# Four small PE steps of a planned transformer layer are queued some products later

## The chip, the cores and the metric

The kernel runs on one core of a Trainium2 chip. Its engines work side by side, each through a queue of its own in the order in which the program wrote it: PE (TensorE, matrix products; its weight loads are listed apart as PEld), DVE (VectorE), ACT (ScalarE), POOL (GpSimd), and SP (SyncE), which issues most of the transfers from and to HBM. An engine waits on a semaphore where an instruction needs another engine's result, and everything behind that instruction in its queue waits too. The metric is the device time of one execution in microseconds (us); lower is better.

## The reference, cut to what matters

One layer over 512 tokens of width 2048, all in float32:

```
h    = rms_norm(x, norm1_g) * (1 + sc1) + sh1            # sc1, sh1, ... = silu(c) @ w_ada + b_ada
proj = h @ w_in                                          # q, k, v, iq, ik, iw | r, k, v, w, a, g
att  = dsa_sparse_attention(...)    # 8 heads; a score picks the top 128 keys of each query
rwkv = rwkv7_time_mix(...)          # 16 heads of 64; a recurrent state over the 512 tokens
x    = x + gt1 * (concat(att, rwkv) @ w_out)
h2   = rms_norm(x, norm2_g) * (1 + sc2) + sh2
out  = x + gt2 * ((silu(h2 @ w_ffn_gate) * (h2 @ w_ffn_up)) @ w_ffn_down)
```

The queries and keys of the attention, and the keys of the recurrence, are normalised per head, which needs a sum of squares over a head's 128 or 64 columns.

## The kernel before, in words

**The big products.** Activations lie transposed (features on partitions, 512 tokens along a row). Each weight tile is split into a high part `whi` (cast by ACT) and a low part `wlo` (difference by DVE), each activation likewise, and three products (high by high, low by high, high by low) go into one sum `acc` (or `vacc`). A list of jobs gives these main products: the projections by `w_in`, then `w_out`, then the three FFN matrices. Before each job `run_jobs` (line 266) has SP load a tile three jobs ahead, and ACT and DVE split half tiles four ahead. The program holds 10032 main products; below, "main product 1086" counts them in program order.

**The planner.** All else is written as generators, the *streams*: `prep` (line 650, eight pairs of recurrent heads), `solve` (780, on DVE), `scan` (826), `post` (914), the rest of the `w_ada` product on DVE (967, tile `wad`), the key score and its top-k on DVE (1066, `idx_stream`), `norm_qk` (1138) and the heads (1168). `drive` (line 288) lets the job list write three main products, then gives each stream a turn. A planner with a clock per engine estimates when each tile will be ready; a stream that calls `until(tile)` gets no further until the planner's PE clock has passed that estimate plus `SLACK`, 0.5. So the planner, on estimates, decides behind how many main products a small PE step stands. Where a job may not be written yet, nothing but streams is written.

**The steps of the change.** `colsum` (line 525) sums columns on DVE: a STREAM_TRANSPOSE into `tr`, a TENSOR_REDUCE into `sums`. `spread` (531) brings the sums across partitions by small PE products into `pst`. `prep` does so once for each of 8 pairs, `norm_qk` once for each of 16 q and k heads, with a rope on DVE between the sums and the products. `prep` later builds `work` on DVE and transposes it on PE (`pT`). `scan` goes through 8 chunks of 64 tokens for each of two groups of heads, and each chunk needs the one before: PE makes `p1` from the chunk's tiles `ch` and the state `SSd`; ACT and DVE copy it into `Rs`; PE makes `p2` from `Rs` and `tt`; DVE and ACT copy that into `ch`; PE makes `p3` and the output `po`; DVE adds `p3` to the state `S` and makes the next `SSd`. In the profile p1, p2 and p3 are all called `p`, told apart by what they read: `p<-SSd,arc` and `p<-ch` with it (p1), `p<-R,tt` (p2), `p<-ch x16` right ahead of `po` (p3).

**The gate on the q and k jobs.** Attention heads start only when the scan of both groups has ended and the top-k is done. Until then at most four (later six) q and k tiles may wait:

```
1265    def few():
1266        return len(qk) <= (6 if len(scanned) == 2 else 4)
1269            group_T(win, h * 128, TWO, ALLK, 4, hrhs, evac_qk("q", h), need=few)
```

The tiles q0, q1, k0, k1, q2 and q3 make six, so the job behind main product 2448 is not written until the scan has ended. The `w_out` jobs behind main product 3048 need all heads.

Of the kernel before, what the change touches and what calls it, by code (L numbers as in the profile page):

```python
# [48 lines left out]
def layer_kernel(ctx, tc, x, c, positions, w_ada, b_ada, norm1_g, w_in, q_norm_g, k_norm_g,  # L49
# [8 lines left out]
    ready = {}  # L58
# [4 lines left out]
    def nm(ap):  # L63
        t = getattr(ap, "tensor", None)
        return getattr(t, "name", None)
# [67 lines left out]
    def now():  # L133
        return clk["pe"]

    SLACK = 0.5
    PACE1, PACE, PACE2 = 3.6, 1.9, 3.0

    def until(*aps):

        t = max(ready.get(nm(a), 0.0) for a in aps) + SLACK
        while now() < t:
            yield

    def room(key="dve", lim=3.0):
        while clk[key] - now() > lim:
            yield

    def banks(n):

        while True:
            for k in [k for k, v in psread.items() if v is not None and v <= now()]:
                del psread[k]
            if len(psread) + n <= 4 and side["pe"] <= SIDE:
                return
            yield
# [16 lines left out]
    def G(name="g", dt=F32):  # L173
        return gpool.tile([128, 512], dt, name=name, tag="g")

    def B(name="b", dt=F32):
        return bpool.tile([128, 2048], dt, name=name, tag="b")
# [4 lines left out]
    def SM(name="sm"):  # L182
        return spool.tile([128, 16], F32, name=name, tag="sm")
# [4 lines left out]
    def PS(name="ps"):  # L188
        t = psp.tile([128, 512], F32, name=name, tag="ps")
        psread[nm(t)] = None  # L190
        return t

    def mm(o, l, r, start=True, stop=True):
        PE.matmul(o, l, r, start=start, stop=stop)
# [187 lines left out]
    def ada_take(kind, c0, k):  # L382
        while (kind, c0, k) not in ada_t:
            yield
        t, last = ada_t.pop((kind, c0, k))
        yield from until(t)
        return t, last
# [137 lines left out]
    def colsum(dst, t):  # L525

        u = G("tr")
        V.transpose(u, t)
        V.tensor_reduce(dst, u.rearrange("p (b c) -> p b c", c=32), axis=mybir.AxisListType.X, op=OP.add)

    def spread(ps, parts, col=C_MOD):

        pv = parts.rearrange("p (j a) -> p a j", a=4)
        for a in range(4):
            mm(ps[32 * a:32 * a + 32], cst[:, col:col + 32], pv[:, a, :])
# [114 lines left out]
    def prep(j):  # L650
# [15 lines left out]
        sm = SM("sums")  # L666
# [1 line left out]
        sg, at = G("sg"), G("at")  # L668
        A.activation(sg, pw, AF.Tanh, scale=0.5, bias=der[:, D_HW + j:D_HW + j + 1])
        A.activation(at, pa, AF.Tanh, scale=0.5, bias=der[:, D_HA + j:D_HA + j + 1])  # L670
        yield from until(sm)
        yield from banks(1)
        pst = PS("pst")
        for h in range(2):
# [35 lines left out]
        work = B("work").rearrange("p (u f) -> p u f", f=1024)  # L710
# [11 lines left out]
        V.tensor_tensor(BK[:, :, 1, :], v3(kf), v3(e2), op=OP.mult)  # L722
        SP.dma_start(ars[:, :, j, :].rearrange("c p f -> p c f"), work[:, 0, :].rearrange("p (c f) -> p c f", f=128))
        V.scalar_tensor_tensor(rt, rt, v2[:, R_RK + j:R_RK + j + 1], kf, op0=OP.mult, op1=OP.mult)
        yield from until(work)
        BKf = work[:, 1, :].rearrange("p (c f) -> p c f", f=128)
        ARf = work[:, 0, :].rearrange("p (c f) -> p c f", f=128)
        for half in range(2):
# [97 lines left out]
    def scan(g):  # L826
# [8 lines left out]
        def load(cI):  # L835
            ch = B("ch").rearrange("p (j f) -> p j f", f=512)
            ar = G("arc")
            hs = slice(cI % 2 * 64, cI % 2 * 64 + 64)
            SP.dma_start(ch[:, :, 0:384], pk[cI, :, js, 0:384])
            SP.dma_start(ch[64:128, :, 384:512], pk[cI, 64:128, js, 384:512])  # L840
            P.memset(ch[0:64, :, 384:512], 0.0)
            SP.dma_start(ar.rearrange("p (j f) -> p j f", f=128), ars[cI, :, js, :])
            SP.dma_start(tt[hs].rearrange("s (q t) -> s q t", t=C), xts[g, :, cI * 8:cI * 8 + 8, :])
            loads[cI] = ch, ar.rearrange("p (j f) -> p j f", f=128)
# [3 lines left out]
        SSd, tt, Rs = G("SSd"), G("tt"), G("R")  # L848
# [5 lines left out]
        for cI in range(NC):  # L854
            if cI + 1 < NC:
                load(cI + 1)
            ch, ar = loads.pop(cI)
            rs = slice(cI % 2 * 64, cI % 2 * 64 + 64)
            yield from until(ch, ar, SSd)
            yield from banks(1)  # L860
            p1 = PS("p1")
            for jj in range(4):
                if cI:
                    mm(p1[0:64, jj * 128:(jj + 1) * 128], ar[:, jj, 0:64], SSd[:, jj * 128:(jj + 1) * 128], True, False)
                for h in range(2):
                    mm(p1[0:64, jj * 128 + h * 64:jj * 128 + h * 64 + 64], ch[:, jj, h * 128:h * 128 + 64],
                       ch[:, jj, 384 + h * 64:384 + h * 64 + 64], cI == 0, cI == 0 or h == 1)
            yield
            A.copy(Rs[rs, 256:512], p1[0:64, 256:512])
            V.tensor_copy(Rs[rs, 0:256], p1[0:64, 0:256])  # L870
            yield from until(Rs, tt)
            yield from banks(1)
            p2 = PS("p2")
            for jj in range(4):
                for h in range(2):
                    o = jj * 128 + h * 64
                    mm(p2[0:64, o:o + 64], tt[rs, (h * 4 + jj) * 64:(h * 4 + jj + 1) * 64], Rs[rs, o:o + 64])
            yield
            V.tensor_copy(ch[0:64, 0:2, 384:512], p2[0:64, 0:256].rearrange("p (j f) -> p j f", f=128))
            A.copy(ch[0:64, 2:4, 384:512], p2[0:64, 256:512].rearrange("p (j f) -> p j f", f=128))  # L880
            yield from until(ch)
            yield from banks(2)
            po = PS("po")
            if cI + 1 < NC:
                p3 = PS("p3")
                for jj in range(4):
                    for h in range(2):
                        mm(p3[h * 64:h * 64 + 64, jj * 64:(jj + 1) * 64], ch[:, jj, 256 + h * 64:256 + h * 64 + 64],
                           ch[:, jj, 384 + h * 64:384 + h * 64 + 64])
            for jj in range(4):  # L890
                if cI:
                    mm(po[:, jj * 64:(jj + 1) * 64], SSd[:, jj * 128:(jj + 1) * 128], ar[:, jj, 64:128], True, False)
                for h in range(2):
                    mm(po[h * 64:h * 64 + 64, jj * 64:(jj + 1) * 64], ch[:, jj, 384 + h * 64:384 + h * 64 + 64],
                       ch[:, jj, h * 128 + 64:h * 128 + 128], cI == 0, True)
            yield
            if cI + 1 < NC:
                ec = e1c[:, cI, js].unsqueeze(2).broadcast_to([128, 4, 64])
                p33 = p3[:, 0:256].rearrange("p (j v) -> p j v", v=64)
                if cI:  # L900
                    V.tensor_tensor(S03, p33, S03, op=OP.add)
                else:
                    V.tensor_copy(S03, p33)
                for h in range(2):
                    hs = slice(h * 64, h * 64 + 64)
                    V.tensor_tensor(SS4[hs, :, h, :], S03[hs], ec[hs], op=OP.mult)
                P.tensor_tensor(S03, S03, ec, op=OP.mult)
            A.copy(O[:, :, cI * C:(cI + 1) * C], po[:, 0:256].rearrange("p (j t) -> p j t", t=C))
            yield
# [115 lines left out]
    def rope(t, rows, tab, mask):  # L1025
        cs, sn = tab
        u = G("u")
        V.stream_shuffle(u[rows], t[rows], mask)
        V.tensor_tensor(u[rows], u[rows], sn[rows], op=OP.mult)
        V.tensor_tensor(t[rows], t[rows], cs[rows], op=OP.mult)  # L1030
        V.tensor_tensor(t[rows], t[rows], u[rows], op=OP.add)
# [106 lines left out]
    def norm_qk(kind, h, t, sq):  # L1138
        yield from until(sq)
        yield from room()  # L1140
        sm = SM("sums")
        colsum(sm, sq)
        rope(t, slice(0, 32), att["qtab"], QM)
        yield from until(sm)
        yield from banks(1)
        pst = PS("pst")
        spread(pst[:, 0:4], sm)
        yield
        st, rr = SM("st"), rpool.tile([128, 4], F32, name="rr", tag="rr")
        V.tensor_scalar(st[:, 0:4], pst[:, 0:4], 1.0 / 128, NORM_EPS, op0=OP.mult, op1=OP.add)  # L1150
        P.tensor_tensor(rr, st[:, 0:4], mhalf.broadcast_to([128, 4]), op=OP.pow)
        if kind == "q":
            P.tensor_scalar(rr, rr, 128.0 ** -0.5, 0.0, op0=OP.mult, op1=OP.add)
            qstat[h] = rr
            return
        yield from until(rr)
        yield from banks(1)
        prb = PS("prb")
        for tt in range(NT):
            PE.transpose(prb[:, tt * 128:(tt + 1) * 128], rr[:, tt:tt + 1].broadcast_to([128, 128]), ident)  # L1160
        yield
        V.tensor_tensor(t, t, prb, op=OP.mult)
        head_queue.append(h)
# [399 lines left out]
```

## Time and profile before

| | |
|---|---|
| time, median of 3 runs | 2717.81 us (2717.71 to 2721.15) |
| the profiled execution's own time | 2725.45 us |
| its span, first to last instruction | 2723.7 us |
| PE busy | 2657.4 us (98%) |
| DVE busy | 1459.7 us (54%) |
| ACT busy | 807.9 us (30%) |
| mean granted TensorE clock | 0.985 of full speed |

PE is the engine that bounds the kernel, and its main products are the same before and after. What a change of order can move is PE's idle time, and the share of the time that PE's clock is at half speed. A row of the timeline gives start and duration in us, the engine, the operation and its tiles, and in brackets how long the engine was idle before and what ended that. The listed duration of one product, about 0.39 us, is longer than its distance to the next, about 0.227 us, since products overlap.

### The profile page before, as it was taken

What the parts mean: (1) busy time and instruction counts of PE and PEld (TensorE: products, weight loads), DVE (VectorE), ACT (ScalarE), POOL (GpSimd) and SP (SyncE); (2) the same over time, 40 slices, a digit from 0 to 9 for tenths busy, and PEclk for the clock granted to TensorE, in tenths of its full rate; (3) what the DMA queues carried; (4) which work ended last, traced back from release to release, by engine and by line L of the source; (5) the groups of instructions that cost most, each with busy time, mean ns of one, the idle gap of its engine ahead of it and who ended that gap; (6) DMA issues with size and microseconds to landing.
All of it is one profiled execution on the core that took longest, in us unless ns stands there. A gap on an engine that the chain in (4) does not pass through costs nothing.

```text
span 2723.7 us, 35144 instructions
## 1 busy us (share of the span) xinstructions
PE 2657.4 (98%) x13351; PEld 2107.0 (77%) x13351; DVE 1459.7 (54%) x2541; ACT 807.9 (30%) x1475; POOL 180.2 (7%) x194
## 2 busy tenths in 40 slices
PE   7999999999998999999999899999999999999999
PEld 4477777767776787887888788888888888888887
DVE  3367779979778778754555432323333232332333
ACT  3244333323322334323422222222222222222222
POOL 2001101100021223110000000000000000000000
PEclk8999999999998999998999999999999999999999
DMA  9966675574663344751555333333333332323332
GB/s 323 333 215 196 214 189 178 163 180 126 163 211 117 126 158 151 247 174 55 192 171 178 100 98 97 97 97 97 99 95 99 95 100 94 100 94 98 96 105 97
DMA packets 383258, 396.10 MB, mean 145 GB/s; under 512 B 52506, under 2 KB 332384, under 8 KB 383088
## 3 DMA queue, kind: packets, MB, share of 16 engines
q1 hardware_dynamic: 380848, 387.25, 45.6%
q0 software_dynamic: 2096, 6.34, 0.7%
q8 instruction: 105, 1.72, 0.3%
q14 instruction: 65, 0.53, 0.1%
q10 hardware_dynamic: 144, 0.26, 0.0%
HBM read 358.13 MB, written 35.65 MB: 145 GB/s over the span
## 4 chain that ended last, share of the span: by engine, by line
PE 90%; DVE 4%; DMA 2%; issue 2%; SPq 1%; ACT 1%; POOL 0%; POOLq 0%; DVEq 0%; ACTq 0%
PE acc L127 77%; PE vacc L127 4%; PE po L127 2%; PE p L127 2%; PE adaacc L127 1%; SPq L127 1%; DMA wada<-in_w_ada_dram 1%; DVE wlo L127 1%; PE dot L127 1%; DMA wraw<-in_w_in_dram 1%; PE pl L127 1%; PE pA L127 0%; PE prb L127 0%; PE pgt L127 0%; DMA xtok<-in_x_dram 0%
## 5 line engine op out<-in xcount | busy, mean ns | idle before, releaser
L127 DVE TENSOR_TENSOR wlo<-wraw,whi 128x512 fp32r<-128x512 f32 (+2 forms) x868 | 580.1, 674 | 1015.1 <-ACT whi L127 1010.7
L127 PE MATMUL acc<-hhi,whi 128*128 128x512 f32 (+1 forms) x2256 | 909.8, 403 | 8.3 <-ACT hhi L127 6.2
L127 ACT CAST whi<-wraw 128x512 fp32r<-128x512 f32 (+2 forms) x868 | 519.1, 604 | 1312.2 <-PE acc L127 1201.8
L127 PE MATMUL acc<-hhi,wlo 128*128 128x512 f32 (+1 forms) x2256 | 882.7, 391 | 1.6 <-DVE wlo L127 1.5
L127 PE MATMUL acc<-hlo,whi 128*128 128x512 f32 (+1 forms) x2256 | 883.0, 391 | 1.2 <-DVE hlo L127 0.8
L127 PEld LDWEIGHTS acc<-hhi,whi 128*128 128x128 f32 (+1 forms) x2256 | 423.8, 188 | 128.3 <-issue 28.6
L127 PEld LDWEIGHTS acc<-hhi,wlo 128*128 128x128 f32 (+1 forms) x2256 | 424.1, 188 | 94.3 <-DVE wlo L127 2.9
L127 PEld LDWEIGHTS acc<-hlo,whi 128*128 128x128 f32 (+1 forms) x2256 | 424.4, 188 | 92.5 <-issue 6.1
L127 PE MATMUL acc<-act,whi 128*128 128x512 f32 x1408 | 436.8, 391 | 0.0
L127 PEld LDWEIGHTS acc<-act,whi 128*128 128x128 f32 x1408 | 264.4, 189 | 54.4
L127 PE MATMUL acc<-act,wlo 128*128 128x512 f32 x704 | 274.9, 390 | 0.0
L127 DVE SCALAR_TENSOR_TENSOR wad<-wad,cact 128x512 f32<-128x512 f32 x240 | 185.4, 772 | 0.9
L127 PEld LDWEIGHTS acc<-act,wlo 128*128 128x128 f32 x704 | 132.7, 188 | 27.7
L127 PE MATMUL acc<-mhi,whi 128*128 128x512 f32 x256 | 100.4, 392 | 0.0
L127 PE MATMUL acc<-mhi,wlo 128*128 128x512 f32 x256 | 99.7, 389 | 0.0
L127 PE MATMUL acc<-mlo,whi 128*128 128x512 f32 x256 | 99.6, 389 | 0.0
L127 DVE SCALAR_TENSOR_TENSOR x<-acc,gt,x 128x512 f32<-128x512 f32 x80 | 57.2, 750 | 40.6 <-PE acc L127 40.6
L127 DVE TENSOR_TENSOR X<-X,stmp 128x462 f32<-128x462 f32 (+21 forms) x138 | 70.7, 512 | 4.9
L127 DVE TENSOR_TENSOR stmp<-X,N 128x462 f32<-128x462 f32 (+21 forms) x138 | 70.0, 507 | 3.9 <-DMA N<-nab 2.2
L127 PEld LDWEIGHTS acc<-mhi,wlo 128*128 128x128 f32 x256 | 48.1, 188 | 10.0
L127 PEld LDWEIGHTS acc<-mhi,whi 128*128 128x128 f32 x256 | 48.1, 188 | 9.9
L127 PE MATMUL vacc<-whi,hhi 128*128 128x512 f32 x128 | 55.7, 435 | 0.0
(255 smaller groups left out, 1970.8 us busy)
## 6 DMA issues: line engine op xcount, KB each, us to landing
wad<-in_w_ada_dram SPq DMA_DIRECT2D x256, 256.0 KB, 4.1
wraw<-in_w_in_dram SPq DMA_DIRECT2D x107, 512.0 KB, 5.0
wraw<-in_w_ffn_down_dram SPq DMA_DIRECT2D x88, 512.0 KB, 3.5
wraw<-in_w_ffn_up_dram SPq DMA_DIRECT2D x84, 512.0 KB, 3.5
wraw<-in_w_ffn_gate_dram SPq DMA_DIRECT2D x80, 512.0 KB, 3.5
wada<-in_w_ada_dram SPq DMA_DIRECT2D x128, 256.0 KB, 6.7
wraw<-in_w_out_dram SPq DMA_DIRECT2D x32, 512.0 KB, 3.6
pk<-pack SPq DMA_DIRECT2D x16, 768.0 KB, 4.3
```

The source lines that it names most:

```text
L127: return f(*args, **kw)
```

## The change

`until` gets an extra delay `more`, and four calls use it: 3.0 ahead of `pst` in `prep`, 1.5 ahead of the transposes of `work`, 0.7 ahead of the scan's p2, 3.0 ahead of `pst` in `norm_qk`.

```
-    def until(*aps):
+    def until(*aps, more=0.0):
-        t = max(ready.get(nm(a), 0.0) for a in aps) + SLACK
+        t = max(ready.get(nm(a), 0.0) for a in aps) + SLACK + more
...
-        yield from until(sm)
+        yield from until(sm, more=3.0)
         yield from banks(1)
         pst = PS("pst")
...
-        yield from until(work)
+        yield from until(work, more=1.5)
...
-            yield from until(Rs, tt)
+            yield from until(Rs, tt, more=0.7)
             yield from banks(1)
             p2 = PS("p2")
...
-        yield from until(sm)
+        yield from until(sm, more=3.0)
```

No instruction of the computation is added or taken away; the order changes on every engine.

**First place: DVE at the column sums of the fifth pair.** On PE the products `pst` of the fifth pair stand behind main product 1086 in both kernels. On DVE `stmp` and `X` are the steps of `solve`, `v` the evacuation of a projection. Before:

```order
L127 TENSOR_TENSOR stmp<-X,N 128x228
L127 TENSOR_TENSOR X<-X,stmp 128x4x57
L127 TENSOR_TENSOR wlo<-wraw,whi 128x512
L127 TENSOR_TENSOR stmp<-X,N 128x224
L127 TENSOR_TENSOR X<-X,stmp 128x4x56
L127 TENSOR_TENSOR stmp<-X,N 128x275
L127 TENSOR_TENSOR X<-X,stmp 128x5x55
L127 SCALAR_TENSOR_TENSOR wad<-wad,cact 128x512
L127 SCALAR_TENSOR_TENSOR v<-acc,v_231,v 128x511 x2
L127 TENSOR_TENSOR wlo<-wraw,whi 128x512
L127 STREAM_TRANSPOSE tr<-sq 128x512
L127 TENSOR_REDUCE sums<-tr 128x16
```

The same place on DVE now:

```order
L127 TENSOR_TENSOR wlo<-wraw,whi 128x512
L127 SCALAR_TENSOR_TENSOR wad<-wad,cact 128x512
L127 SCALAR_TENSOR_TENSOR v<-acc,v_231,v 128x511 x2
L127 TENSOR_TENSOR wlo<-wraw,whi 128x512
L127 STREAM_TRANSPOSE tr<-sq 128x512
L127 TENSOR_REDUCE sums<-tr 128x16
L127 TENSOR_TENSOR stmp<-X,N 128x63
L127 TENSOR_TENSOR X<-X,stmp 128x63
L127 TENSOR_TENSOR stmp<-X,N 128x62
L127 TENSOR_TENSOR X<-X,stmp 128x62
```

The first steps of `solve`, of which 18 stood ahead of these sums, now all stand behind them. The `wlo` ahead of the sums is the 100th split in both; SP's transfers of `N`, which follow transfers of `nab` that they must wait for, now stand behind two more weight tiles.

**Second place: PE behind main product 2448.** The numbers in `p_...` are buffer numbers; each `p<-R,tt` is the p2 of one chunk. Before:

```order
L127 MATMUL p_8000<-R,tt 64x64 x8
L127 MATMUL acc<-hhi,whi 128x512
L127 MATMUL acc<-hlo,whi 128x512
L127 MATMUL acc<-hhi,wlo 128x512
L127 MATMUL p_8044<-ch 64x64 x8
...
L127 MATMUL pst<-sums,cst 32x4 x8
L127 MATMUL p_8102<-SSd,arc 64x128
...
L127 MATMUL p_8129<-R,tt 64x64 x8
...
L127 MATMUL pm<-O,cst 128x512 x2
L127 MATMUL acc<-hhi,whi 128x512
```

The same place now, from main product 2448 to the next (rows of `po`, `p<-ch` and `pst` left out):

```order
L127 MATMUL acc<-hhi,wlo 128x512
L127 MATMUL p_7843<-R,tt 64x64 x8
...
L127 MATMUL p_7935<-SSd,arc 64x128
...
L127 MATMUL p_7968<-R,tt 64x64 x8
...
L127 MATMUL p_8034<-SSd,arc 64x128
...
L127 MATMUL p_8064<-R,tt 64x64 x8
...
L127 MATMUL p_8123<-SSd,arc 64x128
...
L127 MATMUL p_8153<-R,tt 64x64 x8
...
L127 MATMUL pm<-O,cst 128x512 x2
```

Before, the end of the second group's seventh chunk and all of its eighth stood between main products 2448 and 2449. Now the end of its fifth chunk, from p2 on, and all of chunks six, seven and eight stand there.

**Third place: PE behind main product 3048.** `pl` are a head's logits, `pt` the transposes of its weights, `po` its output. Before, with 15 main products between the last head's `pl` and the first `pt`:

```order
L127 MATMUL pl<-k,q 128x256
L127 MATMUL acc<-mhi,whi 128x512
...
L127 MATMUL acc<-mhi,wlo 128x512
L127 MATMUL pt<-cst,lt 128x128 x10
L127 MATMUL po<-lt,vh 128x128 x10
L127 MATMUL pt<-cst,lt 128x128 x10
L127 MATMUL po<-lt,vh 128x128 x10
```

Now:

```order
L127 MATMUL acc<-mhi,wlo 128x512
L127 MATMUL pl<-k,q 128x512
L127 MATMUL pl<-k,q 128x384
L127 MATMUL pl<-k,q 128x128
L127 MATMUL pl<-k,q 128x256
L127 MATMUL pt<-cst,lt 128x128 x10
L127 MATMUL po<-lt,vh 128x128 x10
L127 MATMUL pt<-cst,lt 128x128 x10
L127 MATMUL po<-lt,vh 128x128 x10
```

The last head's logits now stand behind main product 3048, right ahead of the transposes of the head before it.

## Rows read from the trace of the kernel before

**Rows 1.** Waits of PE over the span: us in total, times, longest us

```profile
PE pst L127 <- DVE sums L127: 6.9, 2, 3.8
...
PE p L127 <- DVE R L127: 2.0, 2, 1.1
...
PE acc L127 <- DVE wlo L127: 1.5, 1, 1.5
...
PE pst L127 <- DVE O L127: 1.1, 1, 1.1
```

**Rows 2.** Timeline of SP, 340 to 366: start us, us, queue, operation, tiles

```profile
345.40 6.84 SPq L127 DMA_DIRECT2D N<-nab  x2
```

**Rows 3.** Timeline of DVE, 361 to 376; idle before and its releaser in brackets

```profile
362.05 0.69 DVE L127 TENSOR_TENSOR wlo<-wraw,whi 128x512 fp32r<-128x512 f32 x1 [7.03 <-ACT whi L127]
...
373.91 0.69 DVE L127 TENSOR_REDUCE sums<-tr 128x16 f32<-128x512 f32 x1
```

**Rows 4.** Stretches: us, busy of PE, PEld, DVE, ACT, POOL, granted clock, DMA

```profile
374.40:381.20 6.80, 6.46 (x30) 5.14 (x31) 6.63 (x15) 0.62 (x1) 0.51 (x1) 0.50 0.40 119
...
869.00:893.00 24.00, 14.47 (x86) 10.83 (x87) 21.87 (x49) 2.62 (x6) 3.52 (x5) 0.51 0.55 176
```

**Rows 5.** Chain of waits in order of time: start us, us, what

```profile
375.14 11.25 PE acc L127 x36
...
849.30 0.62 PE p L127 x16
849.92 2.52 PE po L127 x24
...
856.89 1.95 PE p L127 x24
...
1102.25 102.72 PE acc L127 x453
```

**Rows 6.** Timeline of PE between main products 2448 and 2449

```profile
864.72 0.40 PE L127 MATMUL acc<-hhi,wlo 128*128 128x512 f32 x1
...
873.08 0.29 PE L127 MATMUL pst<-sums,cst 128*32 128x4 f32 x8 [3.76 <-DVE sums L127]
876.92 0.66 PE L127 MATMUL p<-SSd,arc 128*64 128x128 f32 x2 [3.55 <-issue]
...
881.47 1.97 PE L127 MATMUL p<-R,tt 64*64 64x64 f32 x16 [0.90 <-DVE R L127]
...
891.67 1.42 PE L127 MATMUL acc<-hhi,whi 128*128 128x512 f32 x1
```

**Rows 7.** Timeline of DVE in the same stretch

```profile
863.74 0.69 DVE L127 MAX8 m<-score 128x8 f32<-128x512 f32 x1
...
865.13 0.41 DVE L127 COPY ch<-p 64x256 f32<-64x256 f32 x1
865.46 0.54 DVE L127 MAX8 m<-score 128x8 f32<-128x384 f32 x1
...
866.58 0.42 DVE L127 MAX8 m<-score 128x8 f32<-128x256 f32 x1
...
867.44 0.70 DVE L127 STREAM_TRANSPOSE tr<-sqq 128x512 f32<-128x512 f32 x1
...
875.52 0.41 DVE L127 TENSOR_TENSOR S<-p,S 128x256 f32<-128x256 f32 x1
...
876.85 0.23 DVE L127 TENSOR_SCALAR st<-pst 128x4 f32<-128x4 f32 x2
...
883.70 0.74 DVE L127 SCALAR_TENSOR_TENSOR wad<-wad,cact 128x512 f32<-128x512 f32 x1
884.36 0.41 DVE L127 COPY ch<-p 64x256 f32<-64x256 f32 x1
```

**Rows 8.** Timeline of PE around main product 3048

```profile
1089.14 2.32 PE L127 MATMUL pl<-k,q 128*128 128x512 f32 x8
...
1102.00 0.47 PE L127 MATMUL acc<-mhi,whi 128*128 128x512 f32 x1
```

## The prediction

> **What bounds the kernel now.** I read the page first: PE is busy nearly all the time, and the chain of waits is mostly main products. So the waits of PE come next, since a later place in PE's queue can only win back what PE waits there. They are few [rows 1]: 6.9 us for column sums, in two places, 1.1 us for a `pst` behind other DVE work, 2.0 us for p2 behind the copies of R, in two places. The transposes of `work` have no row in that view. All of it is 10 us of 2723.7, so the waits that the four delays aim at bound any gain, and the question is what the later order makes late. For that I compared the two orders with the timelines of the stretches where they differ most.
>
> **The change part by part.**
>
> *The transposes of `work` (1.5 later).* PE waits for nothing there, so nothing is won: 0 us. The main products ahead of them hide what was hidden already.
>
> *`pst` in `prep` (3.0 later).* Seven of eight pairs show no wait. The eighth case is the fifth pair, with 3.1 us (6.9 less 3.8 [rows 1]). Its `pst` does not move against the main products; what changes is DVE ahead of it. Before, SP stood 6.84 us at the transfers of `N` [rows 2], a weight tile came late, DVE stood 7.03 us at its split, and then worked through 18 steps of `solve` before it came to the sums at 373.91 [rows 3]. Now these steps stand behind the sums, and two more weight tiles are fetched ahead of `N`, so the split ahead of the sums has its data. Then the 3.1 us go. [...] Together -6.2 us. If another wait comes in its place, 0.
>
> *p2 in the scan (0.7 later).* One of its two waits (1.1 us [rows 1]) is the first chunk's, where p2 now stands 36 instead of 33 main products behind p1: three products of 0.227 us, -0.7 us. The other, 0.90 us [rows 6], has no main product left to hide behind.
>
> *`pst` in `norm_qk` (3.0 later).* The wait of 3.76 us [rows 6] stands behind main product 2448, where there is no product to be queued ahead, so it stays or turns into another. The 1.1 us and the 1.5 us for a `wlo` nearby [rows 1] fall after it, where DVE was loaded with norms and `post`; I take 2.0 of these 2.6 us to go, bounds 0 and -2.6.
>
> *What the delays do to the scan.* Each delay is small, but `prep` runs eight times in a row and the scan's 16 chunks follow one another, so the scan falls back against the main products. The gate behind main product 2448 stands still in the list and opens only when the scan has ended. Before, the end of chunk seven and chunk eight stood there without cover: from 864.72 to 891.67, 26.95 us [rows 6], with DVE busy 21.87 of 24 us and the clock at 0.51 [rows 4]. Now two whole chunks more stand there, and the p2 of chunk five.
>
> How long is that bare stretch? DVE's queue fills it with rounds of the top-k, and the scan's copies stand among them, so I add up DVE's queue with distances from [rows 7]: a round over 512 keys 1.39 us (863.74 to 865.13), over 384 1.12, over 256 0.86; a copy 0.33; two norms of q 8.08 (867.44 to 875.52); S and the next SSd 1.33; a `wad` step 0.66. Counting the changed order from main product 2448:
> - end of chunk five: about 0.2 to the copy of R, rounds of 256 and 512 (2.25), two norms (8.08), copy (0.33), then 384, 256, `wad`, 512 and a small step (4.1), S and SSd (1.33): 16.3 us;
> - chunk six: four rounds of 384, three of 256, three of 512 (11.2), one `wad` (0.66), two copies (0.66), S and SSd (1.33), a transpose and reduction with a small step (1.5, an estimate from the norms): 15.4 us;
> - chunk seven: three rounds of each width (10.1), three `wad` (2.0), two copies (0.66), S and SSd (1.33): 14.1 us;
> - chunk eight to the next main product: as before, 876.92 to 891.67, 14.75 us [rows 6].
>
> Sum 60.5 us, 33.6 more than before. But two chunks' PE work no longer stands among main products elsewhere: p1 1.95, p3 0.62, po 2.52 [rows 5] and p2 1.0 (half of 1.97, which was at half clock [rows 6]) are 6.1 us a chunk, twice, and one p2: 13.2 us. Net +20.4 us. From below: if DVE held nothing up, a bare chunk would be PE's own chain at half clock, 4.55 from p1 to p2 (876.92 to 881.47), 1.97 for p2, 0.7 for two copies, 1.1 for p3 (0.62, slower), 1.33 for S and SSd: 9.7 us, so 2 x (9.7 - 6.1) = +7 us. From above: 16.3 us for each, 2 x 10.2 + 4 for the longer end of chunk five = +24. I take 20.4, because the copy of `ch` at 884.36 started as the `wad` step of 883.70 ended [rows 7], although p2, 1.97 us from 881.47, was done by 883.4 [rows 6]: a copy does wait for the top-k and `wad` work ahead of it.
>
> [...]
>
> *The last heads.* From the last head's `pl` at 1089.14 to the next main product at 1102.00 are 12.9 us, with 15 main products (3.4 us) inside [rows 8]. Now these stand ahead of `pl`. If the head's own chain through DVE, ACT and POOL sets the 12.9 us, 3.4 us are lost; if PE's work did, nothing. `pt` of the head before must still follow its own chain, now with less cover, so I take +3.0.
>
> Sum: 20.4 + 3.0 - 6.2 - 0.7 - 2.0 = +14.5 us. The profiled execution's 2725.45 becomes 2740.0. That execution lies 7.6 us above the median of the runs, 2717.81, so on the median I forecast 2732.3.
>
> **Rivals.** A measurement of this kernel can tell about 0.2%, 5.4 us, from no change.
> - *A: the chain, not DVE, paces the bare chunks.* Then +7 + 3.0 - 8.9 = +1, 2719, no change. For it: PE's part is slow there at half clock. Against it: DVE busy 21.87 of 24 us.
> - *B: faster.* The gate stays shut longer, but the top-k and `post` work done meanwhile on DVE no longer holds PE up afterwards, and all the waits named go, 8.9 us. It decides if the bare stretch costs no more than the PE work that it takes over, about 6.1 us a chunk: then 2709. Against it: p1 and p2 alone, with the copies between, already take 4.55 + 1.97 us there.
> - *C: worse.* The later scan meets new waits: a transfer of `ch` ahead of a chunk, `pst` in new places, or a clock that falls in the gap behind main product 3048, where it had not fallen. [...]
> - *D: the delays do not do what they say.* A `pst` can be held by the planner's count of PSUM banks, as that of the fifth pair seems to be. The moved scan shows that the order does change, so this only shrinks single gains.
>
> **How the numbers follow.** Main case 0.67 (2732, by itself 2726 to 2739), A 0.12, B 0.06, C 0.15; D is within these. The range 2720 to 2746 leaves out B, half of A and the far end of C. Slower by over 0.2%: the main case, C and a little of A, 0.85; within 0.2%: 0.09; faster: 0.06.
>
> **What the new profile would show.** Right: behind main product 2448 a bare stretch of about 60 us with three p1 in it, at half clock, DVE over nine tenths busy; no wait of `pst` near 372 and full clock behind it; a new wait ahead of `pt` near the last heads. Wrong: the bare stretch under 45 us; DVE idle in it; new waits of 3 us or more elsewhere; or waits between 900 and 1100 that go by much more than 2 us.

## The result and the profile after

| | before | after |
|---|---|---|
| median of the runs of this comparison | 2717.76 us (2716.13 to 2721.15) | 2752.66 us (2749.93 to 2756.19, 4 runs) |
| the profiled execution | 2725.45 us | 2756.19 us |

The ratio is 1.0126, 95% interval 1.0114 to 1.0138: 34.9 us slower. The direction was forecast; 14.5 us were, and 2752.66 lies outside the range of 2720 to 2746.

The page's busy time of PE is 2666.2 us, against 2657.4 before, though the products are the same; the mean granted clock was 0.981 against 0.985 of full speed. PE's waits, as in [rows 1], are other ones now (us in total, times, longest):

```profile
PE p L127 <- DVE ch L127: 13.8, 4, 6.7
...
PE p L127 <- DVE R L127: 4.2, 3, 2.2
...
PE po L127 <- ACT lt L127: 2.9, 1, 2.9
PE pst L127 <- DVE sums L127: 2.5, 1, 2.5
PE acc L127 <- DVE mlo L127: 2.5, 1, 2.5
...
PE pst L127 <- DVE R L127: 2.3, 1, 2.3
```

The column sums went from 6.9 to 2.5 us, as hoped; p3 behind the copies `ch`, 0.5 us before, costs 13.8.

To place the loss I took the start of each main product by its number in program order and subtracted. The third column comes from a second profiled execution of the kernel before (below), which at 2717.64 us is a typical one. The profiled execution of the changed kernel was the slowest of its four, 3.5 us above their median, so the last column's sum of 38.2 lies that much over the 34.9:

| main products | first profile of before | second | after | forecast difference | after less first | after less second |
|---|---|---|---|---|---|---|
| up to 1086 | 371.2 | 370.3 | 369.4 | 0 | -1.8 | -0.9 |
| 1086 to 1100 | 9.6 | 7.1 | 3.6 | -6.2 | -5.9 | -3.5 |
| 1100 to 2448 | 483.9 | 481.0 | 476.5 | -13.9 | -7.5 | -4.5 |
| 2448 to 2449 | 26.95 | 26.96 | 63.03 | +33.6 | +36.1 | +36.1 |
| 2449 to 2700 | 97.3 | 96.8 | 93.7 | -2.0 | -3.6 | -3.1 |
| 2700 to 3048 | 105.5 | 105.5 | 110.1 | 0 | +4.6 | +4.6 |
| 3048 to 3049 | 7.5 | 7.5 | 17.0 | +3.0 | +9.5 | +9.5 |
| behind 3049 | 1615.1 | 1614.1 | 1614.1 | 0 | -1.0 | 0 |
| sum | | | | +14.5 | +30.4 | +38.2 |

The bare stretch on PE, which answers [rows 6] (timeline: start, us, tiles, idle before and its releaser):

```profile
849.49 0.40 PE L127 MATMUL acc<-hhi,wlo 128*128 128x512 f32 x1
...
860.54 1.15 PE L127 MATMUL p<-ch 128*64 128x64 f32 x16 [6.73 <-DVE ch L127]
...
866.36 0.69 PE L127 MATMUL p<-SSd,arc 128*64 128x128 f32 x2 [0.31 <-DVE SSd L127]
...
876.77 1.15 PE L127 MATMUL p<-ch 128*64 128x64 f32 x16 [3.42 <-DVE ch L127]
...
882.63 0.66 PE L127 MATMUL p<-SSd,arc 128*64 128x128 f32 x2 [0.58 <-PE po L127]
...
897.38 0.66 PE L127 MATMUL p<-SSd,arc 128*64 128x128 f32 x2 [0.58 <-PE po L127]
...
912.52 1.21 PE L127 MATMUL acc<-hhi,whi 128*128 128x512 f32 x1
```

Three p1 stand in it, as forecast, and the pieces between them can be read off: 16.9 us for the end of chunk five (forecast 16.3), 16.3 for six (15.4), 14.75 for seven (14.1), 15.1 for eight (14.75). p3 waits 6.73 and 3.42 us for copies that stand behind norms and top-k steps on DVE, as DVE's rows show. One thing the forecast had not: the state's next step `SSd` waits for the output product `po`, 0.53 us here, 0.60 and 0.57 in the next two chunks:

```profile
859.48 0.68 DVE L127 TENSOR_TENSOR q<-q,u 32x512 f32<-32x512 f32 x1
860.08 0.41 DVE L127 COPY ch<-p 64x256 f32<-64x256 f32 x1
...
865.45 0.85 DVE L127 TENSOR_TENSOR SSd<-S,e1c 64x256 f32<-64x256 f32 x2 [0.53 <-PE po L127]
...
875.85 0.54 DVE L127 MATCH_REPLACE8 score<-m,score 128x384 f32<-128x384 f32 x1
876.31 0.41 DVE L127 COPY ch<-p 64x256 f32<-64x256 f32 x1
```

The stretches, which answer [rows 4] (us, busy of PE, PEld, DVE, ACT, POOL, granted clock, DMA share, GB/s). After, from main product 2130 to 2265, on to 2400, a part of that, then the bare stretch, 2700 to 3048, 3048 to 3049, and a part of that:

```profile
710.30:760.07 49.77, 49.77 (x384) 40.37 (x383) 29.41 (x68) 14.85 (x31) 4.19 (x7) 1.00 0.91 256
760.07:830.02 69.95, 67.65 (x432) 50.67 (x431) 48.55 (x94) 13.87 (x28) 16.57 (x17) 0.93 0.42 134
822.00:828.80 6.80, 6.80 (x30) 5.21 (x29) 6.52 (x12) 0.00 (x0) 2.06 (x2) 0.56 0.39 113
849.49:912.52 63.03, 39.92 (x302) 32.45 (x301) 55.48 (x134) 7.19 (x17) 5.18 (x9) 0.60 0.41 126
1006.22:1116.34 110.12, 105.14 (x563) 84.67 (x562) 84.73 (x165) 43.90 (x90) 22.07 (x22) 0.98 0.47 154
1116.34:1133.32 16.98, 12.78 (x70) 11.05 (x69) 10.93 (x23) 5.46 (x16) 6.16 (x8) 0.80 0.58 195
1125.00:1131.80 6.80, 6.08 (x28) 6.08 (x29) 3.70 (x7) 2.06 (x4) 1.75 (x3) 0.50 0.73 266
```

The second profile of before, 2130 to 2265, on to 2400, the bare stretch, and 2449 to 2545:

```profile
715.64:792.91 77.27, 77.27 (x561) 58.29 (x559) 58.46 (x128) 17.64 (x37) 14.08 (x15) 0.98 0.76 221
792.91:839.84 46.93, 46.93 (x344) 37.01 (x343) 39.12 (x80) 12.30 (x24) 6.14 (x9) 1.00 0.53 155
858.39:885.35 26.96, 16.91 (x126) 12.73 (x125) 25.58 (x59) 4.47 (x10) 3.52 (x5) 0.63 0.50 156
885.35:921.89 36.54, 36.54 (x167) 27.65 (x166) 28.34 (x61) 11.08 (x22) 11.50 (x11) 0.99 0.35 108
```

After, DVE is busy 29.41 of 49.77 us between 2130 and 2265 (59%), before 58.46 of 77.27 (76%). PE never waits there, so nothing looks wrong; but of the 48 MAX8 steps of the top-k, counted by their start, only 20 come before main product 2448, against 34 before. Between 2265 and 2400 PE now waits 2.30 us and runs at 0.56 of full clock from 822.0 to 828.8, where before it had no wait and 1.00 throughout:

```profile
821.20 0.29 PE L127 MATMUL pst<-sums,cst 128*32 128x4 f32 x8 [2.30 <-DVE R L127]
```

The last heads, which answer [rows 8], on PE and then on ACT:

```profile
1116.34 0.39 PE L127 MATMUL acc<-mhi,wlo 128*128 128x512 f32 x1
1116.57 2.32 PE L127 MATMUL pl<-k,q 128*128 128x512 f32 x8
...
1123.64 1.16 PE L127 MATMUL po<-lt,vh 128*128 128x128 f32 x8 [2.94 <-ACT lt L127]
1125.72 2.93 PE L127 MATMUL po<-lt,vh 128*128 128x128 f32 x12 [0.92 <-DVE lt L127]
...
1133.32 0.47 PE L127 MATMUL acc<-mhi,whi 128*128 128x512 f32 x1
```

```profile
1120.83 0.72 ACT L127 ACTIVATE lt<-lt,s 128x512 f32<-128x512 f32 x1 [4.12 <-POOL lt L127]
...
1123.03 0.83 ACT L127 COPY lt<-pt 128x512 f32<-128x512 f32 x2
```

`po` of the last head but one waits 2.94 us for a copy of its `pt` that stands on ACT behind the last head's exponentials, 1120.83 to 1123.03. The exponentials had themselves waited 4.12 us for a tile from POOL. Behind the wait of `po` the clock is at 0.50 from 1125.0 to 1131.8.

### The profile page after: what moved, and what is told of

It is laid out like the page before. It is cut to its first block, busy times and chain, and to the rows that moved or that the text cites. A ratio compares the mean times of both kernels' runs of the same rounds, so it can differ in the third digit from the quotient of the medians.

```text
span 2754.4 us, 35134 instructions
## 1 busy us (share of the span) xinstructions
PE 2666.2 (97%) x13351; PEld 2115.4 (77%) x13351; DVE 1461.6 (53%) x2541; ACT 807.4 (29%) x1475; POOL 171.5 (6%) x194
## 4 chain that ended last, share of the span: by engine, by line
PE 57%; issue 1%; DVE 1%; ACT 0%; POOL 0%; POOLq 0%; DVEq 0%; ACTq 0%
PE acc L127 57%; PE fin L127 0%; PE po L127 0%; DVE hx L127 0%; DVE wad L127 0%; ACT hhi L127 0%; POOL ssum L127 0%; DVE hlo L127 0%; DVE x L127 0%; PE pt L127 0%; ACT lt L127 0%; DVE gate L127 0%; ACT act L127 0%; DVE wlo L127 0%; PE prb L127 0%
## 5 line engine op out<-in xcount | busy, mean ns | idle before, releaser
L127 PEld LDWEIGHTS acc<-mlo,whi 128*128 128x128 f32 x256 | 48.4, 189 | 12.8 <-DVE mlo L127 2.9
L127 PEld LDWEIGHTS acc<-mhi,wlo 128*128 128x128 f32 x256 | 48.5, 189 | 10.2
```

Source lines behind the costliest of these rows:

```text
L127: return f(*args, **kw)
```

## The experiments

Fifteen runs. The theory tested first, T, was the prediction's: what counts is how many scan steps stand bare behind main product 2448. Each text names its theory and its rival by a letter. All ratios are against the kernel before, with 95% intervals.

**Each delay alone** (three of the four `more=` set to 0).

> Only the delay of 3.0 ahead of pst in prep; the other three are 0. Behind main product 2448 stand, as before, the end of chunk seven and chunk eight. Theory T (a later order costs through the scan chunks that stand bare behind main product 2448, some 9 us each, and through the last heads): no bare chunk more, so no loss, 2711 to 2719. Rival R (each delay costs where it stands, eight pst and what follows them, so the parts add up to the whole of +35 us): 2724 to 2732.

> Only the delay of 1.5 ahead of the transposes of work. Behind main product 2448 now stand p2 of chunk six and all of chunks seven and eight, one chunk more than before; the last heads stand almost as before. PE waited nowhere at these transposes. Theory T: one bare chunk more, +9 to +12 us, 2727 to 2730, although no wait of PE was touched. Rival R (a delay costs by its own steps): transposes that nobody waited for, with 1.5 us for each of 8 pairs hidden behind main products, cost nothing, 2716 to 2720.

> Only the delay of 0.7 ahead of p2. Behind main product 2448 stand p2 of chunk seven, which stood at 2445 before, and chunk eight: no whole chunk more. Theory T: 2716 to 2722, since 16 delays of three products each are hidden until the scan's end passes the gate. Rival R (the delay is paid 16 times): 16 x 0.7 = +11, 2729.

> Only the delay of 3.0 ahead of pst in norm_qk. Nothing changes ahead of main product 2448, and chunk eight stands bare as before. The last head's pl stand 6 instead of 15 main products ahead of the pt behind main product 3048. Theory T: 0 to +4 us, 2717 to 2722, all of it at the last heads. Rival R: the largest part of the +35 us, since 16 heads are delayed by 3.0 each, 2735 or more.

| kept | median us | ratio | 2448 to 2449, us |
|---|---|---|---|
| prep, 3.0 | 2732.60 | 1.0056 (1.0041 to 1.0071) | 23.3 |
| work, 1.5 | 2741.00 | 1.0084 (1.0069 to 1.0099) | 46.2 |
| p2, 0.7 | 2731.63 | 1.0050 (1.0035 to 1.0065) | 31.8 |
| norm, 3.0 | 2721.73 | 1.0018 (1.0009 to 1.0028) | 25.2 |

T fits only the last. Three delays were each dearer than it allowed; for `prep` and p2 the rival came within 3 us, for `work` it missed by 21, for `norm_qk` by 13. T's place was right for `work`: its bare stretch grew by 19.2 us, but the stretch from 1100 to 2448 gave back only 3.5. For p2 a part arose ahead of the gate: 2130 to 2265 took 82.2 us, against 77.3 in the second profile of before (below), with PE newly idle for 4.24 of them. The differences from the median of before, 2717.71, add to more (14.9 + 23.3 + 13.9 + 4.0 = 56 us) than the whole change costs. The delay in `prep` put nothing more behind 2448, yet cost 15 us. Its rows show where, at the next gate: 2449 to 2545 took 54.5 us, against 36.5 in that second profile. The job behind main product 2544 is not written until a head has started, and a head needs its norms and the top-k from DVE; the last top-k step started at 941.8 us, against 899.0.

```profile
924.16 0.29 PE L127 MATMUL pst<-sums,cst 128*32 128x4 f32 x8 [3.49 <-DVE sums L127]
928.08 0.29 PE L127 MATMUL pst<-sums,cst 128*32 128x4 f32 x8 [3.62 <-DVE sums L127]
931.90 2.09 PE L127 MATMUL prb<-cst,rr 128*128 128x128 f32 x8 [3.53 <-POOL rr L127]
```

**The kernel before, profiled again; the scan alone later; no delay for the last heads.**

```
-            yield from until(pk, ars, xts)                    # scan
+            yield from until(pk, ars, xts, more=12.0 * g)     # late12; 30.0 * g in late30
...
-        yield from until(sm, more=3.0)                        # norm_qk
+        yield from until(sm, more=3.0 if h < 6 else 0.0)      # after_h6, in the changed kernel
```

> The kernel before, word for word in its instructions, profiled once more. The execution on which the prediction rests took 2725.45 us, 7.6 above the median, and the profile with only the norm_qk delay, whose order is the same up to main product 2280, was 5.2 us earlier at main product 1806. Theory V (the waits and half clock at 371 to 381 and 589 to 600 belong to that one execution): this profile takes 2714 to 2721 us, with one or both of these clock falls gone, so the prediction's -6.2 us for the column sums of the fifth pair was never there in the median. Rival: the same waits and falls again, 2723 to 2727 us.

> The kernel before, with none of the four delays; instead the loads of the second scan group wait 12 longer in the planner's count. All is unchanged up to main product 2139; behind main product 2448 stand p2 of chunk six and all of chunks seven and eight: one chunk more. The last heads are better covered than before (their last pt behind 3048 alone). Theory T: one bare chunk more and the tail longer, 15 to 17 us bare less 6 of PE work, +9 to +12, 2726 to 2730. Rival R (the loss comes from the delayed steps themselves, wherever they stand): 2715 to 2720.

> The kernel before, with none of the four delays; the loads of the second scan group wait 30 longer in the planner's count. Behind main product 2448 stand the end of chunk five and chunks six, seven and eight, as in the changed kernel. The last heads have 18 and more main products of cover. Theory T: the bare stretch is 60 to 64 us as in the changed kernel, less 13 of PE work taken over, +20 to +24 us, and the last heads without the loss of the changed kernel: 2736 to 2742. Rival R: 2715 to 2720, and the changed kernel's loss lies in the four delays.

> The changed kernel, but the delay in norm_qk is 0 for the last two heads. The same order as the changed kernel up to main product 2868; the last heads' pl stand behind 3012 and 3036 instead of 3033 and 3048, so 12 main products lie again between the last pl and its pt. Theory H (the changed kernel loses 9.5 us behind main product 3048, since two heads' chains stand there one upon the other): 5 to 9 us faster than the changed kernel, 2744 to 2748. Rival (PE's own work set that stretch): within 2 us of the changed kernel, 2751 to 2755.

The second profile took 2717.64 us, and the fall of the clock at 589 was gone (1.00 from 580 to 600, against 0.51 from 589.6 to 599.8 in the first), as V said. The wait at 372 is 1.82 us there, against the 3.1 that the forecast took, and main products 1086 to 1100 took 7.1 us instead of 9.6. Three more kernels have the order of before up to there: 8.1 (norm_only), 5.2 (late12) and 7.5 us (late30).

```profile
372.51 0.31 PE L127 MATMUL pst<-sums,cst 128*32 128x4 f32 x16 [1.82 <-DVE sums L127]
```

In the changed kernel the same product has no wait:

```profile
369.71 0.31 PE L127 MATMUL pst<-sums,cst 128*32 128x4 f32 x16
```

late12: 2725.16 us, 1.0027 (1.0017 to 1.0037), bare stretch 42.1 us. late30: 2737.02 us, 1.0082 (1.0062 to 1.0102), bare stretch 54.8 us, with the same scan steps bare as in the changed kernel:

```profile
845.29:900.05 54.76, 38.77 (x303) 31.47 (x301) 45.56 (x105) 7.18 (x17) 5.14 (x9) 0.60 0.41 128
```

Against before at 2717.43, a late second half of the scan, with no other delay, costs 7.7 and then 19.6 us: the time of late30 fell into T's range, that of late12 just short of its own, though T had put the bare stretch of late30 at 60 to 64. The 19.6 are somewhat over half of the 34.9. The stretch from 1100 to 2448, which the same steps left as in the changed kernel, took 467.2 us in late30: 13.8 less than in the second profile, where the changed kernel saved only 4.5.

after_h6: 2752.28 us, 1.0131 (1.0115 to 1.0148): no gain that these runs can tell, where 5 to 9 us were expected. The stretch from 3048 to 3049 fell from 17.0 to 12.3 us, but 2700 to 3048 rose from 110.1 to 112.6; what is left lies within what executions of one kernel differ by.

**Top-k cut, gate opened.** Theory Q: DVE's queue paces the bare chunks. Theory G: a shut gate is what costs.

```
-        for rnd in range(16):                                      # idx_stream
+        for rnd in range(1):                                       # before_notopk, after_notopk
...
-        return len(qk) <= (6 if len(scanned) == 2 else 4)
+        return len(qk) <= 6                                        # before_gate6, prep_gate6
```

> The kernel before, with 1 of the 16 rounds of the key score's top-k left out of none but kept alone (15 rounds of MAX8 and MATCH_REPLACE on DVE are left out, so the output is not the layer's). It is the base for the next kernel; p2 of the last two chunks stands behind main product 2448, as before. Theory Q (DVE's queue paces the bare chunks, since copies stand behind top-k rounds there): bare stretch from 27 to 20 us or less, the whole 2703 to 2712. Rival P (PE's own steps and the hops to the next engine pace it, at half clock): bare stretch 24 to 27 us, the whole 2712 to 2718.

> The changed kernel with 15 of the 16 top-k rounds left out in the same way; p2 of the last three chunks stands behind main product 2448 (of the last four, and the end of the fifth, with the top-k). Compare with the kernel before without these rounds. Theory Q: a bare chunk takes about 10 us, so the one chunk more in the bare stretch costs 10 less the 6 of its own PE work, about 4 us, and the change as a whole 12 to 20 us instead of 35. Rival P: a bare chunk still takes 14 to 16 us, the change as a whole 24 to 35 us.

> The kernel before, where the fifth and sixth q and k tiles no longer wait for the end of the scan; only the gate for a seventh stays, behind main product 2544. The last p2 stands behind product 2514, with main products around it, and nothing of the scan behind a gate. Theory G (a shut gate with bare chunks behind it is what costs): the bare stretch of 27 us at 2448 goes, and about 12 to 15 us of it comes back as a wait for the first head at 2544, so 2704 to 2716. Rival L (the loss only moves to the next gate, since the first head needs the scan's end, the top-k and its norms, one after the other): 2718 to 2732.

> The same opened gate with the one delay of 3.0 in prep. The last p2 stands behind product 2499, earlier than with the opened gate alone; the first head's logits again right at the gate of 2544. With the delay and the gate as it was the cost was 15 us. Theory G: the delay costs only what it does at a gate, and the scan no longer ends at one, so within 5 us of the opened gate without delay. Rival L: the first head comes later again, since norms and top-k are late: 10 to 16 us above the opened gate without delay.

before_notopk: 2725.73 us, 1.0028 (1.0017 to 1.0038); after_notopk: 2740.34 us, 1.0079 (1.0064 to 1.0094). Between them the change costs 14.6 us instead of 34.9, inside Q's 12 to 20; but one p2 less stands bare there, three and not four, so not all of that is the pace. In the kernel before Q missed: its bare stretch fell only from 27.0 to 25.0 us, as P said, and not to 20 or less. What PE waits for there is mostly the norms of two heads (3.76 and 3.55 us [rows 6]), which stayed. In the changed kernel without the top-k a bare chunk without norms, from its p1 to the next, takes 11.6 us on PE:

```profile
869.97 0.66 PE L127 MATMUL p<-SSd,arc 128*64 128x128 f32 x2 [0.58 <-PE po L127]
...
881.57 0.66 PE L127 MATMUL p<-SSd,arc 128*64 128x128 f32 x2 [0.58 <-PE po L127]
```

In the changed kernel chunks six and seven took 16.3 and 14.75, so 3 to 5 us of each were DVE's top-k, and 11.6 is the chain with `po` in it, not the 9.7 of the prediction's lower bound. Both theories missed that the kernel before got slower without 15 of 16 rounds. The planner writes another order then: 2700 to 3048 took 117.4 us, against 105.5, with more of the heads' products and longer waits in it.

before_gate6: 2717.67 us, 0.9998 (0.9989 to 1.0008): no difference. The bare stretch is gone, 0.23 us from 2448 to 2449, and 25 us of it come back at the gate of 2544. From 2449 to 2545 (stretch, then two of the waits):

```profile
859.98:921.60 61.62, 53.73 (x306) 38.18 (x304) 53.77 (x117) 13.96 (x26) 14.87 (x15) 0.89 0.30 92
```

```profile
897.19 1.12 PE L127 MATMUL prb<-cst,sq 128*128 128x128 f32 x4 [1.87 <-POOL sq L127]
905.92 0.63 PE L127 MATMUL prb<-cst,sq 128*128 128x128 f32 x4 [3.57 <-DVE O L127]
```

The second profile of before has 36.54 us there; these are 61.62, with DVE busy 53.77. In the second profile DVE is busy 25.58 us in the bare stretch and 28.34 in this one, 53.9 together: as much. prep_gate6 took 2733.64 us, 1.0059 (1.0044 to 1.0074), 16 us above the opened gate alone. G falls both times (the opened gate alone also ended 0.3 us below L's range): in the kernel before, the bare chunks behind 2448 are not a price in themselves. While PE stands there, DVE does work that the next gate needs.

**What DVE owes.** Theory B: the price is DVE's late work ahead of the gates. Rival S: the bare scan steps themselves.

```
-                yield from room("dve", 1.0)                   # top-k
+                yield from room("dve", 2.0)                   # after_room2, before_room2
...
-            yield from until(Rs, tt)                          # scan
+            yield from until(Rs, tt, more=-0.4)               # early_p2
```

> The changed kernel, where the planner lets the top-k run 2.0 instead of 1.0 us ahead of PE on DVE: 33 instead of 17 of the 48 steps of the top-k stand ahead of the 212th split, and the scan's last four chunks from p2 on stand behind main product 2448 (before: the same four). Theory B (what costs behind 2448 is work that DVE still owes there, since it stood idle earlier): the bare stretch falls from 63 us to 50 to 55, the whole 2738 to 2747. Rival S (the bare scan steps themselves cost, whatever DVE owes): the stretch stays at 60 to 66 us, the whole 2750 or more.

> The same in the kernel before: 40 instead of 29 top-k steps stand ahead of the 212th split, and all of the seventh chunk's bare steps come from p2 on, as before, though later by some main products. Theory B: the bare stretch of 27 us falls or stays, and no wait takes its place: 2708 to 2717. Rival S: the seventh chunk stands bare from an earlier step, so 2720 to 2728.

> The kernel before with p2 0.4 earlier (a delay of -0.4 in place of the 0.7): only the last chunk's p2 stands behind 2448, and the top-k is later: 23 of 48 steps ahead of the 212th split, against 29; the first logits stand behind 2547 instead of 2460. Theory B: less bare scan, but what DVE owes then holds the first head up at the gate of 2544, so no gain: 2714 to 2726. Rival S: the bare stretch shrinks to 15 to 20 us and the gain stays: 2706 to 2712.

after_room2: 2738.74 us, 1.0074 (1.0059 to 1.0089), 13.9 below the changed kernel, within B's range; but the bare stretch stayed at 60.5 us, as S said, where B had 50 to 55. The gain came elsewhere (stretches 2130 to 2265, on to 2400, and the bare one):

```profile
710.82:760.60 49.78, 49.78 (x385) 40.37 (x383) 39.09 (x96) 15.61 (x31) 4.19 (x7) 1.00 0.86 244
760.60:820.19 59.59, 59.59 (x405) 45.78 (x403) 49.05 (x105) 13.51 (x27) 13.19 (x15) 1.00 0.48 146
840.98:901.49 60.51, 43.32 (x326) 35.69 (x325) 40.04 (x82) 7.60 (x18) 7.23 (x9) 0.56 0.52 157
```

DVE is busy 39.09 instead of 29.41 us in the first, and 40 of the 48 top-k steps come before 2448 instead of 20; in the second PE waits for nothing and keeps full clock (1.00), 10.4 us shorter; the main product 2448 comes at 841.0 instead of 849.5 (24 small products of one p1, about 2 us, have moved behind it) and 3048 to 3049 takes 8.9 instead of 17.0 us. Within the stretch chunks six and seven take 12.0 and 13.0 us (p1 at 862.51, 874.52, 887.50).

before_room2: 2723.14 us, 1.0016 (1.0007 to 1.0026), bare stretch 37.5 us. All 48 top-k steps came before 2448, the scan was pushed back instead; S was right, B not.

early_p2: 2738.12 us, 1.0078 (1.0061 to 1.0095), where B said at most 2726 and S at most 2712. The bare stretch shrank to 18.4 us and the next stretch, to 2545, grew from 36.5 to 50.7, with DVE busy 17.87 and 41.67 us of them and only 29 top-k steps ahead of 2448:

```profile
870.56:888.94 18.38, 11.77 (x87) 8.48 (x85) 17.87 (x41) 3.69 (x8) 3.37 (x5) 0.67 0.58 173
888.94:939.62 50.68, 39.56 (x191) 29.20 (x189) 41.67 (x87) 10.07 (x17) 11.79 (x10) 0.90 0.31 99
```

B's mechanism is there, and gives back more than the shorter stretch won (14.1 us for 8.6). The rest arose ahead of 2448, which came 12.2 us later than in the second profile. Most of that arose between 1806 and 2130, 11.5 us, with PE idle for 5.0 us of it and 36 more small products; neither theory had it.

No version beat the kernel before; before_gate6 equals it.

## Why the prediction was wrong, point by point

**Where the change acts: right.** The gate behind 2448, the order of steps in it, the low clock (0.60 on the mean), DVE nearly full (55.48 of 63.03 us, 88%, where over nine tenths were forecast) and a wait at the last heads (of `po`, where one ahead of `pt` was forecast) came as forecast. The bare stretch was 63.0 us for 60.5.

**The step that failed: the credit of 13.2 us in "What the delays do to the scan".** It held that PE work which stands bare later is saved among the main products earlier, and put at nothing what the delays do to DVE, and so to PE, in that earlier stretch. With the first p2's 0.7, -13.9 us were to show between 1100 and 2448; -4.5 did against the typical profile (-7.5 against the first; after_h6, with the same order there, saved 6.3 against the typical one). The size of the work was right: in late30, which has none of the four delays, the same 176 small products left that stretch, and it was 13.8 us shorter, with DVE busy 47.76 of 60.99 us (78%) between 2130 and 2265. In the changed kernel they left it too, but waits and a lower clock took their place. PE's waits of over 0.1 us there sum to 10.4 us, against 5.4 in the second profile (the longest new one is the 2.30 of `pst` behind DVE's R). Time below full clock, summed over short stretches as length times the missing share, is estimated to cost 6.8 us against 3.4 (the longest fall is that of 822.0 to 828.8, at 0.56; after_h6 had the same wait of 2.30 us ahead of it and no fall there). Together 8.4 of the missing 9.4 us. That the losses hang on DVE's late work is supported by after_room2: with the top-k further ahead the wait and the fall between 2265 and 2400 were gone, and 2448 came 8.5 us earlier, about 2 of them by the moved p1. The prediction had DVE's load as the pace of the bare stretch only, not as something that the delays put off before it.

**The last heads: +3.0, measured +9.5.** The mechanism, cover lost, was right; unseen were ACT's queue, where one head's exponentials stand ahead of the other's copies (`po` waited 2.94 us), and the fall of the clock (0.50 from 1125.0 to 1131.8). Rival C had named that fall. But after_h6 shows that winning 4.7 us back there need not shorten the whole by as much.

**From 2700 to 3048: 0, measured +4.6.** PE's waits there grew from 3.4 to 5.0 us, with 2.50 for a split of `mlo` new, a fall of the clock (0.50 from 1102.0 to 1104.0) costs 1.7 by the same estimate, and 30 of the heads' small products moved in from the stretch ahead (8 others moved out, behind 3048). None of it was looked for. late30, with none of the delays, has +6.0 there, so a late scan alone can bring such a loss.

**The column sums: -6.2.** The mechanism was right: the wait went, and the stretch lost 5.9 us against the profile used. In the second profile only 3.5 were there to win, in the three other kernels with this order 1.6 to 4.5. The forecast took a gain read in one execution off the median of others, and that execution was 7.6 us above it. The half of the term that is for the clock, 3.1 us, no run shows: by length times the missing share, an estimate, the first profile lost 3.4 us there (6.80 us at 0.50 [rows 4]), the second 1.7 (10 us at 0.83, from 370 to 380) and the changed kernel nothing (1.00 from 369 to 381).

**Norms, 942 to 948: -2.0.** -3.1 over 2449 to 2700, but by luck. The two waits named went, and others came in their place: 1.45 us of `pt` behind DVE's O and 1.06 of `prb` behind POOL, 2.5 us in sum against 2.6 in the second profile. The stretch is shorter since 30 small products of a head moved out of it. In norm_only, where this delay stands alone, PE waits for nothing there and the stretch is 2.2 us shorter, as forecast.

**The rivals.** A falls: the bare chunks took 14.75 and 16.3 us, the chain alone 11.6, not 9.7, since SSd waits for `po` (0.53 to 0.60 us idle on DVE in the changed kernel); so DVE's queue added to it, and the chain was dearer than A held. B falls. D was not tested by itself. C, at 0.15, is what happened on top of the main case: new waits at `ch` (13.8 us, 0.5 before), `pst` (2.30) and the heads (2.94), and a clock that fell in new places (0.56 from 822.0, 0.50 from 1125.0).

**What stays open.** The share of each delay, since their costs do not add, and why p2, earlier by 0.4, made early_p2 wait ahead of product 2130. That the scan's place carries a part of the loss is shown (late30). That DVE's late work carries another is well supported (after_notopk and after_room2), but both runs also changed the order elsewhere. One number for each is not shown.

## What to carry to other kernels

Where a list of jobs has gates, do not price a delay by the steps that it lays bare alone: ask what the vector engine leaves undone while it waits for them, and follow that to the next gate. Work that was moved out of a busy stretch was not always saved here: the same 176 products left one for a gain of 13.8 us in late30 and, with new waits in it, of 4.5 in the changed kernel. Look for a fall of DVE's busy share in a stretch where PE is still full (here from 76 to 59%). Take a second profile of the same kernel before crediting a gain of a few us to one wait or one fall of the clock.

## What the runs showed of the hardware that was not expected

The same instructions in the same order did not meet the same clock. In the first profile of before, PE's clock stood at 0.51 for 10.2 us where the second has none:

```profile
589.60:599.80 10.20, 10.20 (x35) 7.15 (x34) 8.90 (x15) 3.11 (x6) 0.00 (x0) 0.51 0.10 30
```

```profile
580.00:600.00 20.00, 19.23 (x118) 13.34 (x117) 19.19 (x35) 5.92 (x13) 0.00 (x0) 1.00 0.38 126
```

What PE did before: it waited for the same product of the key score, 1.16 us in the first profile, 0.77 in the second, and there it kept full clock:

```profile
588.97 1.68 PE L127 MATMUL dot<-ik,iq 64*128 64x512 f32 x2 [1.16 <-DVE R L127]
```

```profile
585.64 1.12 PE L127 MATMUL dot<-ik,iq 64*128 64x512 f32 x2 [0.77 <-DVE R L127]
```

10.2 us at 0.51 are 5.0 us lost, of the 7.6 by which the first profile was above the median. The bare stretch, 26.95 and 26.96 us in the two, was the same to a hundredth.
